# A query tile of sixteen heads, asked for once instead of once per head

## Chip, cores and metric

One core of a Trainium2 chip runs the kernel. The metric is the device time of one execution in microseconds (us), as the median of three runs. Lower is better.

## What is computed

The reference is a two-layer backbone over 1024 latent tokens (plus 256 context tokens) of width 1024. Layer 0 mixes neighbourhood attention with mLSTM heads. Layer 1, the last one, is a bidirectional gated linear recurrence (HGRN2) of 16 heads with key and value width 128. Cut to one direction of one head of layer 1, in chunks:

```
b = cumsum(lf)                       # lf = log(f), f the forget gate; k = 1 - f
o = (q * exp(b)) @ S                 # what the state carried into the chunk gives
a = einsum(q, exp(b_t - b_s) * k)    # pairs inside the chunk, s <= t
o = o + a @ v
S = exp(b_last) * S + (k * exp(b_last - b)).T @ v
```

The two directions are added, normalised per head, multiplied by a SiLU gate and projected back.

## The kernel before, in words

Everything is float32. A projection is split into a high and a low part and takes three TensorE matmuls per product (lines 131 to 133, in `dense`).

Layer 1 is a loop over 16 heads (lines 1443 to 1460). A head h consists of these pieces:

- `hg_intra` (from line 1027) makes, from the gates F and the query halves q, the tile K = 1 - F (line 1031), the two sums of keys (1036) and the **query tile Q** (1038). Q has 128 partitions and two rows of 1024 tokens, one for each direction. Four VectorE products fill it: for the token half `hf` = 1 (tokens 512 to 1023) and then `hf` = 0 (tokens 0 to 511), two directions each. Then come seven levels (`hg_level`): TensorE reads Q and keys in strips of 64 by 64 (line 1059), and VectorE multiplies parts of Q and K in place by the gate products (line 1106). The keys of a level are first copied by ScalarE into gksel (line 1089).
- `hg_vz` projects values and the gate z, `hg_close` transposes the keys, `hg_ctx` makes the states that the context leaves.
- `hg_scan` walks over eight chunks c of 128 tokens. For each chunk TensorE adds three matmuls into a PSUM tile "acc": line 1137 with the within-chunk matrix gA, lines 1138 and 1139 with the 128 columns of chunk c of the two rows of Q. VectorE then makes the next forward state (line 1144). After each group of four chunks, ScalarE squares the result (1153), VectorE multiplies it by z into the same columns of gA (1157), and GpSimd normalises (1158).
- `hg_proj` of the next head projects its gates and queries; `hg_out` transposes and stores the result. A few heads also do small sums on GpSimd (`wo_sums`, `y_diff`).

After the loop comes an output projection, whose weights arrive over SyncE's DMA queue.

Tiles come from pools with `self.t(pool, shape, dtype, tag, bufs)` (line 55). A request under a tag with one buffer gets the memory of the earlier tile of that tag only when every instruction that uses the earlier tile is through. Inside one tile the framework keeps account of which instructions read and write which part, and orders those that overlap.

The order of the instructions on each engine isn't written out by hand. The framework plans it while it builds the program, from a model of how long each instruction takes (`schedule_with_timeline_sim=True` in the launch): at each point an engine is given the ready instruction of the best priority. Priority follows the program's order, except that what stands under `urgent()` (the strips and the in-place products of the levels) goes ahead of everything. On the chip each engine then runs its list in that fixed order and waits where an operand isn't there.

Of the kernel before, what the change touches and what calls it, by code (L numbers as in the profile page):

```python
# [10 lines left out]
F32 = mybir.dt.float32  # L11
# [8 lines left out]
P = 128  # L20
D = 1024
KD = D // P
LAT = 1024
# [22 lines left out]
class Prog:  # L46
# [980 lines left out]
    def hg_intra(self, h, st, pool):  # L1027
        nc = self.nc
        F, q = st["F"], st["q"]
        K = self.t(pool, [P, 2, LAT], F32, "gK", 1)  # L1030
        nc.vector.tensor_scalar(out=K, in0=F, scalar1=-1.0, scalar2=1.0, op0=ALU.mult, op1=ALU.add)
        Q = self.t(pool, [P, 2, LAT], F32, "gQ", 1)
        ks = [self.t(pool, [P, 512], F32, "gkn", 4) for _ in range(2)]
        for hf in (1, 0):
            s = slice(hf * 512, (hf + 1) * 512)
            nc.vector.tensor_tensor(out=ks[hf], in0=K[:, 0, s], in1=K[:, 1, s], op=ALU.add)
            for d in range(2):
                nc.vector.tensor_tensor(out=Q[:, 1 - d, s], in0=q[hf], in1=F[:, d, s], op=ALU.mult)
        hv = dict(Q=Q, K=K, T=F, D=self.t(pool, [P, 8, 64], F32, "gD", 1))
        hv["A"] = self.t(pool, [P, 8, P], F32, "gA", 1)  # L1040
        if h == 0:
            self.t(pool, [P, 16], F32, "pad", 1)
        pa = self.ps("s", [P, 8, 64])
        with self.urgent():
            for c in range(8):
                for b in range(2):
                    o = c % 4 * P + b * 64
                    self.strip(pa[:, c, :], b, ks[c // 4][:, o : o + 64], q[c // 4][:, o : o + 64])
        nc.vector.tensor_tensor(
            out=hv["D"], in0=pa, in1=self.lmask[:, 0, :].unsqueeze(1).to_broadcast([P, 8, 64]), op=ALU.mult  # L1050
        )
        for lev in range(7):
            self.hg_level(hv, lev, pool)
        return hv
# [23 lines left out]
    def hg_level(self, H, lev, pool):  # L1078
        nc = self.nc
        n, h = LAT, 1 << lev  # L1080
        nb = n // (2 * h)
        K, Q, A, D, Tt = H["K"], H["Q"], H["A"], H["D"], H["T"]

        pick = lambda t: _skew(t[:, 0, :].rearrange("p (b s i) -> p b s i", s=2, i=h), 2, n)
        out = self.ps("s", [P, 8, 64])
        with self.urgent():
# [5 lines left out]
            for c in range(8):  # L1092
                for b in range(2):
                    o = c * P + b * 64
                    r = out[:, c, :]
                    if lev < 6:
                        r = r.rearrange("p (b s i) -> p b s i", s=2, i=h)
                        lhsT, rhs = ksel[:, o : o + 64], pick(Q)[:, o // (2 * h) : (o + 64) // (2 * h)]
                    else:
                        lhsT = K[:, b, o : o + 64]  # L1100
                        rhs = Q[:, 1 - b, c * P + (1 - b) * 64 : c * P + (2 - b) * 64]
                    self.strip(r, b, lhsT, rhs)
            for t, o, step in ((Q, n + 1, -n - 1), (K, 1, n - 1)):
                v = bass.AP(t.tensor, t.offset, [list(t.ap[0]), [n + h, 2], [2 * h, nb], [1, h]])
# [673 lines left out]
```

## Time and profile before

| | us |
|---|---|
| median of 3 runs | 3375.06 (3374.84 to 3375.25) |
| the profiled execution | 3376.8 |
| its span, first to last instruction | 3375.0 |
| TensorE (PE) busy | 3321.0 |
| VectorE (DVE) busy | 2022.1 |
| ScalarE (ACT) busy | 1402.1 |
| GpSimd (POOL) busy | 661.2 |

The profile is of one execution. PEld is the loading of weights into TensorE, which runs beside the matmuls. A row of a timeline gives the start and the length in us, the engine, the line of the kernel, the operation, what it writes and reads, how many instructions are merged into the row, and in brackets how long the engine was idle before and what it had waited for. Matmuls are pipelined: a row that says 0.28 us may be followed by the next start after 0.11 us. Layer 1's heads run from about 1839 to 3260 us.

### The profile page before, as it was taken

How to read it: one execution, taken by the hardware profiler on the slowest of the kernel's cores; microseconds unless marked ns; L12 is line 12 of the kernel's file. 1: busy time of each engine (PE TensorE's matmuls, PEld its weight loads, DVE VectorE, ACT ScalarE, POOL GpSimd, SP SyncE). 2: the span in 40 equal slices, each digit the busy share in tenths (PEclk: the TensorE clock that was granted, in tenths of full speed). 3: DMA queues.
4: the chain of work that ended last, by engine and by line, in shares of the span. 5: the costliest groups of instructions: out<-in, count | busy, mean ns of one | idle time of the engine just before them, and what ended most of it. 6: DMA issues, size and time to landing. Idle time of an engine off the chain costs nothing. (4 is left out here: it accounts for less than half of the span.)

```text
span 3375.0 us, 64228 instructions
## 1 busy us (share of the span) xinstructions
PE 3321.0 (98%) x24982; PEld 2940.1 (87%) x24982; DVE 2022.1 (60%) x4791; ACT 1402.1 (42%) x3310; POOL 661.2 (20%) x1059
## 2 busy tenths in 40 slices
PE   6999999999999999999999999999999999999999
PEld 5689999888989888898888999988899999989877
DVE  4437666666655566787656555555555555555557
ACT  5335544555544444454454333333333333333343
POOL 2222222222211112221100111122112222321110
PEclk8999999999999999999999999999999999999999
DMA  6622222232233434444652122122122322222366
GB/s 217 234 85 75 80 77 76 76 91 84 71 90 102 147 119 127 131 137 139 215 170 89 45 70 67 60 65 66 62 66 67 79 60 60 76 73 64 79 178 184
DMA packets 315696, 342.02 MB, mean 101 GB/s; under 512 B 32168, under 2 KB 257128, under 8 KB 313344
## 3 DMA queue, kind: packets, MB, share of 16 engines
q1 hardware_dynamic: 269520, 217.85, 21.9%
q0 software_dynamic: 45872, 120.07, 11.6%
q8 instruction: 197, 3.23, 0.4%
q14 instruction: 107, 0.88, 0.1%
HBM read 253.43 MB, written 84.21 MB: 100 GB/s over the span
## 5 line engine op out<-in xcount | busy, mean ns | idle before, releaser
L131 PE MATMUL mm<-hh,wh 128*128 128x512 f32 (+1 forms) x1600 | 583.2, 365 | 0.7 <-ACT gF L958 0.7
L132 PE MATMUL mm<-hl,wh 128*128 128x512 f32 (+1 forms) x1600 | 582.2, 364 | 0.0
L133 PE MATMUL mm<-hh,wl 128*128 128x512 f32 (+1 forms) x1600 | 581.5, 364 | 0.0
L131 PE MATMUL mm<-wh,hh 128*128 128x256 f32 (+1 forms) x1440 | 445.7, 310 | 2.5 <-DVE graw L300 1.4
L132 PE MATMUL mm<-wl,hh 128*128 128x256 f32 (+1 forms) x1440 | 444.7, 309 | 0.0
L133 PE MATMUL mm<-wh,hl 128*128 128x256 f32 (+1 forms) x1440 | 441.9, 307 | 0.0
L131 PEld LDWEIGHTS mm<-hh,wh 128*128 128x128 f32 x1600 | 301.6, 189 | 48.7 <-issue 2.5
L133 PEld LDWEIGHTS mm<-hh,wl 128*128 128x128 f32 x1600 | 301.4, 188 | 44.6 <-issue 0.2
L132 PEld LDWEIGHTS mm<-hl,wh 128*128 128x128 f32 x1600 | 301.7, 189 | 42.1 <-issue 0.2
L131 PE MATMUL mm<-wzh,hh 128*128 128x256 f32 x1024 | 294.5, 288 | 0.0
L133 PE MATMUL mm<-wzh,hl 128*128 128x256 f32 x1024 | 292.0, 285 | 0.0
L132 PE MATMUL mm<-wzl,hh 128*128 128x256 f32 x1024 | 290.2, 283 | 0.0
L131 PEld LDWEIGHTS mm<-wh,hh 128*128 128x128 f32 x1440 | 271.3, 188 | 21.1 <-ACT ev L322 3.4
L132 PEld LDWEIGHTS mm<-wl,hh 128*128 128x128 f32 x1440 | 271.3, 188 | 12.4 <-issue 0.7
L133 PEld LDWEIGHTS mm<-wh,hl 128*128 128x128 f32 x1440 | 271.2, 188 | 12.0 <-issue 0.5
L74 DVE TENSOR_TENSOR wl<-wraw,wh 128x512 fp32r<-128x512 f32 x240 | 167.7, 703 | 159.1 <-ACT wh L73 157.6
L73 ACT CAST wh<-wraw 128x512 fp32r<-128x512 f32 x240 | 147.2, 618 | 226.6 <-PE mm L132 167.2
L131 PEld LDWEIGHTS mm<-wzh,hh 128*128 128x128 f32 x1024 | 193.4, 189 | 2.5
L132 PEld LDWEIGHTS mm<-wzl,hh 128*128 128x128 f32 x1024 | 193.4, 189 | 1.6
L133 PEld LDWEIGHTS mm<-wzh,hl 128*128 128x128 f32 x1024 | 192.9, 188 | 1.2
L1089 ACT COPY gksel<-gK 128x1024 f32<-128x1024 f32 x96 | 110.8, 1154 | 163.9 <-PE s L1059 118.6
L1106 DVE TENSOR_TENSOR gQ<-gQ,gF 128x1024 f32<-128x1024 f32 x112 | 139.9, 1249 | 45.8 <-PE s L1059 44.8
(467 smaller groups left out, 7411.8 us busy)
## 6 DMA issues: line engine op xcount, KB each, us to landing
wraw<-in_wab_dram SPq DMA_DIRECT2D x108, 256.0 KB
wraw<-in_wc_dram SPq DMA_DIRECT2D x96, 256.0 KB
wraw<-yd SPq DMA_DIRECT2D x92, 256.0 KB
wraw<-in_wc_dram SPq DMA_DIRECT2D x128, 128.0 KB
md<-ev POOLq DMA_DIRECT2D x60, 256.0 KB, 2.7
mloz<-md SPq DMA_DIRECT2D x40, 256.0 KB
s<-gyt POOLq DMA_DIRECT2D x36, 256.0 KB, 4.3
adar<-in_wada_dram SPq DMA_DIRECT2D x8, 1024.0 KB
```

The costliest lines, as they stand in the source:

```text
L73: m = nc.scalar.copy(hi, x)
L74: nc.vector.tensor_tensor(out=lo, in0=x, in1=hi.bitcast(F32), op=ALU.subtract)
L131: mm(ps, lhsT=lh(k), rhs=rh(k), start=(start and k == 0), stop=False)
L132: mm(ps, lhsT=lh(k), rhs=rl(k), start=False, stop=False)
L133: m = mm(ps, lhsT=ll(k), rhs=rh(k), start=False, stop=(stop and k == nk - 1))
L1089: m = nc.scalar.copy(ksel.rearrange("p (b s i) -> p b s i", s=2, i=h), pick(K))
L1106: nc.vector.tensor_tensor(out=v, in0=v, in1=tot, op=ALU.mult)
```

## The change

Head 0 asks for the tile under the tag gQ and keeps it in `self.Q`; the other 15 heads use the same tile instead of asking for a new one. No instruction is added or taken away, and the memory is the same one buffer. What differs is on what the first writes of a head depend: not on the end of every use of the tile before, but on the earlier uses of the part that they write.

```diff
         nc.vector.tensor_scalar(out=K, in0=F, scalar1=-1.0, scalar2=1.0, op0=ALU.mult, op1=ALU.add)
-        Q = self.t(pool, [P, 2, LAT], F32, "gQ", 1)
+        if h == 0:
+            self.Q = self.t(pool, [P, 2, LAT], F32, "gQ", 1)
+        Q = self.Q
         ks = [self.t(pool, [P, 512], F32, "gkn", 4) for _ in range(2)]
         for hf in (1, 0):
             s = slice(hf * 512, (hf + 1) * 512)
             nc.vector.tensor_tensor(out=ks[hf], in0=K[:, 0, s], in1=K[:, 1, s], op=ALU.add)
             for d in range(2):
                 nc.vector.tensor_tensor(out=Q[:, 1 - d, s], in0=q[hf], in1=F[:, d, s], op=ALU.mult)
```

## The prediction

> **What bounds the kernel now.** I read the page first: the span and the busy times.
>
> ```profile
> span 3375.0 us, 64228 instructions
> PE 3321.0 (98%) x24982; PEld 2940.1 (87%) x24982; DVE 2022.1 (60%) x4791; ACT 1402.1 (42%) x3310; POOL 661.2 (20%) x1059
> ```
>
> TensorE (PE) is busy 3321.0 of 3375.0 us, so its idle time is 54 us in all. The change neither adds nor removes a matmul. What it can win is therefore at most the part of this idle time that the query tile causes. The table by stretches, for two of the sixteen heads and for one stretch of the last stage, says how much is left inside a head.
>
> ```profile
> 2278.06:2365.84 87.78, 87.15 (x781) 79.30 (x780) 49.98 (x82) 29.25 (x61) 18.23 (x27) 1.00 0.22 70
> 2365.84:2453.63 87.79, 87.17 (x781) 79.32 (x780) 50.08 (x81) 29.48 (x61) 18.32 (x27) 1.00 0.21 66
> ...
> 3280.00:3300.00 20.00, 16.27 (x59) 12.49 (x58) 9.12 (x15) 7.38 (x13) 1.17 (x2) 0.83 1.05 308
> ```
>
> The columns are the stretch, its length, the busy time of PE, PEld, DVE, ACT and POOL, then the clock granted to PE. A head takes 87.8 us, with PE idle for 87.79 - 87.17 = 0.62 us and the clock full. VectorE (DVE) is busy 50 us of it and has 37.7 us to spare. The list of waits, for PE from 1830 us to the end (the heads and the last stage), names what PE waited for:
>
> ```profile
> PE s L1059 <- DVE gQ L1038: 7.2, 12, 0.7
> PE c L131 <- ACT yh L73: 3.7, 1, 3.7
> PE mm L893 <- ACT yh L73: 1.5, 1, 1.5
> PE mm L131 <- ACT gF L958: 0.7, 1, 0.7
> PE c L131 <- DVE gA L1157: 0.6, 1, 0.6
> ```
>
> The first row is the query tile: 12 times, 7.2 us in total, the strips of level 0 waited for the four products that fill Q (line 1038). That is 0.6 us each, the same 0.62 us as in the table. The other rows have nothing to do with the tile. So 7.2 us, or 0.21% of the time, is the stall that this edit addresses. What those products themselves wait for is shown by the answer for the tile gQ:
>
> ```profile
> L1038 DVE TENSOR_TENSOR gQ<-gq,gF x64: 679/685/695, 1839.2 to 3170.8; 128x512 f32<-128x512 f32 x64
> its engine sat idle before it (us, times) until:
>   PE acc L1139: 38.9, 15
> ```
>
> There are 64 products, 4 for each head. In all 15 heads but the first, DVE sat idle (38.9 us in total, 2.6 us each) until line 1139 of the head before had been computed, that is until the scan had read Q for its last chunk.
>
> **The change part by part.** One boundary between heads, in DVE's timeline:
>
> ```profile
> 2368.40 0.35 DVE L1144 SCALAR_TENSOR_TENSOR gS<-gS,gT,s 128x128 f32<-128x128 f32 x1 [1.25 <-PE acc L1139]
> 2369.77 0.35 DVE L1144 SCALAR_TENSOR_TENSOR gS<-gS,gT,s 128x128 f32<-128x128 f32 x1 [1.02 <-PE acc L1139]
> 2371.76 0.69 DVE L1157 TENSOR_TENSOR gA<-acc,gz 128x512 f32<-128x512 f32 x1 [1.65 <-ACT gjk L1153]
> 2373.60 0.69 DVE L1049 TENSOR_TENSOR gD<-s,glm 128x512 f32<-128x512 f32 x1 [1.14 <-PE s L1059]
> 2374.46 0.35 DVE L1144 SCALAR_TENSOR_TENSOR gS<-gS,gT,s 128x128 f32<-128x128 f32 x1 [0.16 <-PE acc L1139]
> 2375.13 0.35 DVE L1144 SCALAR_TENSOR_TENSOR gS<-gS,gT,s 128x128 f32<-128x128 f32 x1 [0.32 <-PE acc L1139]
> 2378.06 2.50 DVE L1038 TENSOR_TENSOR gQ<-gq,gF 128x512 f32<-128x512 f32 x4 [2.58 <-PE acc L1139]
> ```
>
> and in PE's:
>
> ```profile
> 2369.34 0.39 PE L1139 MATMUL acc<-gS,gQ 128*128 128x128 f32 x2
> ...
> 2377.19 0.39 PE L1137 MATMUL acc<-gv,gA 128*128 128x128 f32 x2
> 2377.41 0.39 PE L1138 MATMUL acc<-gS,gQ 128*128 128x128 f32 x2
> 2377.63 0.39 PE L1139 MATMUL acc<-gS,gQ 128*128 128x128 f32 x2
> 2377.78 0.37 PE L131 MATMUL mm<-wzh,hh 128*128 128x256 f32 x1
> ...
> 2379.80 0.28 PE L133 MATMUL mm<-wzh,hl 128*128 128x256 f32 x1
> 2380.70 1.55 PE L1059 MATMUL s<-gQ,gksel 128*64 128x64 f32 x32 [0.62 <-DVE gQ L1038]
> ```
>
> The line 1139 at 2369.34 belongs to chunk 3, that at 2377.63 to chunk 7. Between lie 8.3 us in which columns 0 to 511 of Q are already read for the last time, but the products for them stand behind the last one all the same.
>
> *Is a part of a tile really freed alone?* The trace says so for gA, which is asked for once in each head. Line 1157 writes its first four chunks at 2371.76, while line 1137 still reads its last one at 2377.19: they overlap in nothing, and neither waits for the other. So I take it that with Q kept, the two products of tokens 0 to 511 need only chunk 3, and the two of tokens 512 to 1023 need chunk 7 as now.
>
> *What moves.* Per head, two of four DVE products. DVE's idle stretches before 2378.06 are 1.65, 1.14 and 2.58 us; the four products take 2.50 us, so two take about 1.25. They fit. Nothing else moves by the edit alone: no DMA is issued, no tile of another tag changes its place, and head 0 is as before. The strips of level 0 can then be planned some 1.2 us earlier, and the projection matmuls that stood before them come after them. For PE this is an exchange without price.
>
> *What is gained.* The gap of 0.62 us is an error of the plan: it put about 2.0 us of matmuls (2378.06 to 2379.80, plus 0.28) between the last read of Q and the strips, and the chain on the chip took 2.64 (2378.06 to 2380.70: products 2.50, handing over 0.14). With two products left behind chunk 7, the chain is about 1.25 + 0.14 = 1.39 us. If the plan covers the same share of it as now, 2.02 / 2.64 = 0.77, it puts 1.06 us of matmuls there and a wait of 0.33 us is left. The gain is 0.62 - 0.33 = 0.29 us, times 12 heads = **3.5 us**. The bounds: if the plan's error sits in handing over and not in the products, the wait stays as it is and nothing is won; if the error vanishes with the queue, all 7.2 us go. I take the middle value, since it is scaled from the row of the same operations, and keep both ends. What is late next inside a head is nothing that the waits show: beyond the 0.62 us PE has no idle time there.
>
> *What hides the moved products.* They stand in DVE's queue in the scan. Behind them wait line 1144 (the state, for which line 1139 of the next chunk on PE waits) and line 1157. They cost nothing as long as DVE is idle there anyway, as the rows in brackets show. If one starts just ahead of a 1144, it delays it by up to 0.6 us, and both by 1.25. PE then has the value projection's matmuls to run, unless its fixed order has the scan next.
>
> A row speaks of another price: GpSimd and DVE side by side.
>
> ```profile
> 2381.61 1.04 POOL L1158 TENSOR_TENSOR gA<-gA,gss 128x512 f32<-128x512 f32 x1
> ```
>
> ```profile
> 2382.29 1.45 DVE L1106 TENSOR_TENSOR gQ<-gQ,gF 128x1024 f32<-128x1024 f32 x1 [0.47 <-PE s L1059]
> ...
> 2388.66 1.21 DVE L1106 TENSOR_TENSOR gQ<-gQ,gF 128x1024 f32<-128x1024 f32 x1
> ```
>
> The same product takes 1.45 us where it begins under a GpSimd operation and 1.21 elsewhere. The products that move into the scan can meet the first half's 1158 in the same way. At 0.24 us each, that is at most 0.5 us a head, off PE's path as long as the scan has slack. The Trainium skill, "SBUF — State Buffer", section "Who interferes with whom", has a rule for this: a DVE instruction with two SBUF inputs contends with a GpSimd instruction that reads SBUF, and one of them fully blocks. By it the DVE product could lose the whole rest of the GpSimd operation; the trace shows a loss, but a smaller one than the 0.36 us of overlap that is left at 2382.29.
>
> **The sum.** The profiled execution took 3376.8 us, of which 1.8 lie outside its span; it is 1.7 us above the median of the runs. I take the 3.5 us off the median: 3375.1 - 3.5 = **3371.6 us**.
>
> **The rivals.**
>
> *The wait halves (forecast, 0.40).* As worked out: 3368.5 to 3374.8, likeliest 3371.6.
>
> *The whole bubble goes (0.22).* The plan, with half of the products out of the way, lets PE go on without a gap. Then 7.2 us go: 3367.9, and a little less if the last stage happens to fall better, down to about 3362. For it: the gap is the same 0.6 us in head after head. Against it: nothing in the trace says that the plan errs less on a shorter chain. The Trainium skill, "Perfetto Trace Analysis", section "Identifying the Most-Contended Engine", takes such a gap, repeating on the engine that should be saturated, as a possible sign that there isn't room for the next tile to be allocated. By that rule the whole gap is the tile's and would vanish. The trace agrees in that the gap's products wait for the old tile's last use.
>
> *Nothing happens (0.15).* The order stays, or the wait of the strips hangs on the last product alone. 3375, give or take 1.
>
> *The moved products get in the scan's way (0.18; slower).* The place is DVE's queue between 2369 and 2378 us of this head, the price up to 2 products = 1.25 us a head. It decides from the point at which a product starts less than 0.6 us ahead of a line 1144 whose matmul is next in PE's order. The stretches before 2374.46 and 2375.13 are only 0.16 and 0.32 us long, which speaks for it; the 1.14 to 2.58 us of the others speak against. Fully paid in 15 heads it is 19 us, 3394; for half, 3384. To this case belongs that the plan, made anew, interleaves scan and projections worse.
>
> *The last stage falls differently (0.05).* PE waits 3.7 us once near 3289 (second row of the waits), and in the stretch around it the clock granted is 0.83. Another arrival of the last head can take this away or double it: 4 us either way, so 3368 to 3383 with the rest.
>
> **How the numbers follow.** About 0.2% (6.75 us) is what a measurement of this kernel can tell from no change. Faster by more means below 3368.3: most of the second rival and a little of the forecast, 0.25. Slower by more means above 3381.8: most of the fourth and a little of the last, 0.19. Within: 0.56. The likeliest case's own range is 3368.5 to 3374.8. The range for 8 in 10 reaches to the whole bubble below (3364) and to about half the price of the slower rival above (3384).
>
> **What would show it.** In the changed profile, two of line 1038's products should start right after chunk 3's line 1139, and two after chunk 7's; DVE's idle time before 1038 should fall below 38.9 us. The wait of line 1059 for 1038 should be some 3.5 us in total instead of 7.2, and a middle head last 87.5 us. If the wait is gone altogether, the second rival is right; if all four products still stand together, the third; if waits of PE on 1144 appear or a head takes over 88 us with no more idle time, the fourth. I am wrong from the ground up if heads change by more than 1 us without a change in these waits: then the planner's new order, and not the tile, makes the time.

## The result, and the profile after

The changed kernel takes 3369.36 us (median of 18 runs, 3366.92 to 3374.73), the kernel before 3376.86 us beside it (18 runs, 3374.11 to 3380.89). The ratio is 0.9979, with an interval of 0.9972 to 0.9986: some 7.1 us, or 0.21%, are gone. The forecast was 3371.6 us for a kernel at 3375.1, that is 3.5 us less; the range of 3364 to 3384 held the time. On the chip the whole bubble went, which the prediction had as its second rival at 0.22.

The lines of the changed kernel stand two higher from the products on (the products are line 1040 here, the strips 1061, the scan's matmuls 1139 to 1141, the state 1146). Its profiled execution took 3371.7 us. First its page, span and busy times:

```profile
span 3370.0 us, 64226 instructions
PE 3321.2 (99%) x24982; PEld 2942.5 (87%) x24982; DVE 2032.7 (60%) x4791; ACT 1400.2 (42%) x3310; POOL 660.7 (20%) x1059
```

TensorE does the same work in the same busy time (3321.2 against 3321.0), so what is gone was idle time. VectorE is busy 10.6 us more, with as many instructions as before; the last section tells why. PE's waits from 1830 us on, after:

```profile
PE c L131 <- ACT yh L73: 4.1, 1, 4.1
PE c L131 <- DVE gA L1159: 0.6, 1, 0.6
PE mm L131 <- ACT lasth L73: 0.5, 1, 0.5
PE tr L1073 <- DVE gK L1108: 0.3, 1, 0.3
```

The row with 7.2 us in 12 waits has no successor. No strip waits for the query tile any more. The table by stretches (before the first product of head 0, from there to the first product of head 15, and the rest) says where the span became shorter. Before:

```profile
0.00:1839.21 1839.21, 1803.96 (x12044) 1574.77 (x12045) 1129.73 (x3349) 875.99 (x2234) 365.57 (x640) 1.00 0.39 120
1839.21:3169.02 1329.81, 1322.64 (x11815) 1204.16 (x11814) 754.68 (x1221) 441.73 (x914) 270.11 (x389) 1.00 0.22 64
3169.02:3375.00 205.98, 194.40 (x1127) 161.15 (x1125) 137.72 (x223) 84.40 (x163) 25.56 (x31) 0.98 0.63 173
```

and after:

```profile
0.00:1841.34 1841.34, 1802.56 (x12045) 1574.13 (x12046) 1131.09 (x3349) 875.59 (x2234) 366.67 (x640) 0.99 0.39 120
1841.34:3161.23 1319.89, 1319.63 (x11770) 1201.71 (x11768) 765.39 (x1224) 439.56 (x912) 269.02 (x389) 1.00 0.23 65
3161.23:3370.00 208.77, 199.05 (x1172) 166.70 (x1170) 136.24 (x220) 85.02 (x165) 24.96 (x31) 0.98 0.63 171
```

In the heads PE was idle 1329.81 - 1322.64 = 7.17 us before and 1319.89 - 1319.63 = 0.26 us after. The stretch is 9.92 us shorter: 6.91 of idle time, and 3.01 us of work, 45 PE instructions that the new order runs behind it. The last stretch is 2.79 us longer for them. Both together: 7.13 us less. The first stretch, in which nothing was edited, came out 2.13 us longer in this execution. The last section shows as much between kernels whose TensorE order is the same, so it is taken for chance; it is why the two spans differ by 5.0 us only.

One boundary between heads, DVE's timeline after:

```profile
2364.36 0.35 DVE L1146 SCALAR_TENSOR_TENSOR gS<-gS,gT,s 128x128 f32<-128x128 f32 x1 [1.13 <-PE acc L1141]
2364.81 0.69 DVE L1040 TENSOR_TENSOR gQ<-gq,gF 128x512 f32<-128x512 f32 x1
2365.85 0.35 DVE L1146 SCALAR_TENSOR_TENSOR gS<-gS,gT,s 128x128 f32<-128x128 f32 x1 [0.35 <-PE acc L1141]
2366.11 0.69 DVE L1040 TENSOR_TENSOR gQ<-gq,gF 128x512 f32<-128x512 f32 x1
...
2373.95 1.29 DVE L1040 TENSOR_TENSOR gQ<-gq,gF 128x512 f32<-128x512 f32 x2 [2.30 <-PE acc L1140]
```

Two products now stand in the scan, one ahead of a state product (1146) and one behind it, and only two come after chunk 7. PE at the same place:

```profile
2373.75 0.39 PE L1141 MATMUL acc<-gS,gQ 128*128 128x128 f32 x2
2373.90 0.36 PE L133 MATMUL mm<-wzh,hl 128*128 128x256 f32 x1
...
2377.02 1.58 PE L1061 MATMUL s<-gQ,gksel 128*64 128x64 f32 x32
```

Between chunk 7 and the strips stand 25 matmuls of the value projection, from 2373.90 to 2377.02, so 3.1 us; before, there were 18 in 2.3 us (2377.78 to 2380.08, of which 2.02 lie beside the products), and a gap. The last product ends at 2373.95 + 1.29 = 2375.24. The strips have no wait in brackets, and 1.6 us of slack beyond the hand-over of 0.14. So two things changed at once: the **chain** behind chunk 7 became shorter (two products instead of four), and the **cover** beside it became longer (25 matmuls instead of 18). Which of them took the bubble away is what the experiments had to tell.

### The profile page after: what moved, and what is told of

Read it like the earlier page. It is cut to its first block, busy times and chain, and to the rows that moved or that the text cites. A ratio compares the mean times of both kernels' runs of the same rounds, so it can differ in the third digit from the quotient of the medians.

```text
span 3370.0 us, 64226 instructions
## 1 busy us (share of the span) xinstructions
PE 3321.2 (99%) x24982; PEld 2942.5 (87%) x24982; DVE 2032.7 (60%) x4791; ACT 1400.2 (42%) x3310; POOL 660.7 (20%) x1059
```

## The experiments

Each kernel's ratio is to the kernel before on the same chip, over 11 runs (where not said otherwise), with its interval. The expectations speak of two theories. **A**: a strip's wait is the chain of products that it needs, less the work that the plan has beside it, and the early start of two products brings the chain below that cover. **B**, the prediction's own step: the plan covers a fixed share (0.77) of whatever chain there is. Where an expectation names a further theory (C, D, E), it says what that is. Lines move by a few in each kernel; the products are always the row `gQ<-gq,gF`.

### late: the kept tile, with the early products held back

```diff
             for d in range(2):
-                nc.vector.tensor_tensor(out=Q[:, 1 - d, s], in0=q[hf], in1=F[:, d, s], op=ALU.mult)
+                m = nc.vector.tensor_tensor(out=Q[:, 1 - d, s], in0=q[hf], in1=F[:, d, s], op=ALU.mult)
+                if hf:
+                    last = m
+                else:
+                    self.behind(m, last)
```

`behind` orders an instruction after another one on the same engine. The products of tokens 0 to 511 are put behind the product that fills row 0 of tokens 512 to 1023 (`d` = 1); the other late product stays free.

> The tile is kept, but its two products of tokens 0 to 511 are queued behind the first product of tokens 512 to 1023, so none starts before the last chunk of the scan. Theory A (the wait is the chain of products behind the last chunk minus the matmuls that the plan has ready to put beside it): the chain is again four products, 2.6 us, and from the fifth boundary on only 18 or 19 matmuls, 2.1 to 2.2 us, stand beside it, so PE waits some 0.5 us at 11 boundaries and the time is that of the kernel before, 0.999 to 1.001 of it. Theory C (keeping the tile is itself what helps, by a new plan): 0.998, as in the changed kernel.

Measured: 3369.79 us, 0.9983 (0.9975 to 0.9992). The bubble stayed away, against A as it was worked out. DVE in a middle head of this kernel:

```profile
2552.50 2.50 DVE L1040 TENSOR_TENSOR gQ<-gq,gF 128x512 f32<-128x512 f32 x4 [2.37 <-PE acc L1144]
```

and PE:

```profile
2554.78 1.54 PE L1065 MATMUL s<-gQ,gksel 128*64 128x64 f32 x32
```

All four products are late again, as intended. But the strips start at 2554.78, while the four end only at 2555.00. The edit had changed something else too: one late product now comes last, and only the second half of the strips needs it. In the program the wait is split: the first eight strips wait for three products, the next eight for the fourth. The kernel before has one wait, on all four, for all sixteen strips. The changed kernel has the split wait too: its plan puts row 1 of tokens 512 to 1023 last. The **order** of the products is thus a second possible cause, which neither theory had. `late` therefore doesn't speak for B either, and its result is what theory C gave; `strict` below decides on C.

### early1: one early product instead of two

```diff
-                nc.vector.tensor_tensor(out=Q[:, 1 - d, s], in0=q[hf], in1=F[:, d, s], op=ALU.mult)
+                m = nc.vector.tensor_tensor(out=Q[:, 1 - d, s], in0=q[hf], in1=F[:, d, s], op=ALU.mult)
+                if hf:
+                    last = m
+                elif d == 1:
+                    self.behind(m, last)
```

> As the changed kernel, but only one product may start early; three stand behind the last chunk. Theory A: the chain is 1.9 + 0.14 = 2.0 us, beside it stand 30 matmuls, 3.5 us, so no wait is left and the whole gain is there: 0.998 of the kernel before. Theory B (the prediction's: a fixed share, 0.23, of whatever chain is left is waited for): 0.47 us at 12 boundaries remain, 5.6 us, so the gain is only 1.6 us: 0.9995.

Measured: 3368.04 us, 0.9976 (0.9967 to 0.9985), and no wait of a strip. DVE and PE at a boundary:

```profile
2368.67 1.89 DVE L1040 TENSOR_TENSOR gQ<-gq,gF 128x512 f32<-128x512 f32 x3 [2.40 <-PE acc L1144]
```

```profile
2372.20 1.55 PE L1065 MATMUL s<-gQ,gksel 128*64 128x64 f32 x32
```

The products take 1.89 us, with the hand-over 2.03. By B, 0.23 of it would stay as a wait, 0.47 us a head. There is none: the products end at 2370.56, the strips come 1.6 us later, behind 30 matmuls. B falls with this run. Between early1 and the change (0.9979) no difference can be told.

### dup2: the kept tile, late products done twice

```diff
             for d in range(2):
-                nc.vector.tensor_tensor(out=Q[:, 1 - d, s], in0=q[hf], in1=F[:, d, s], op=ALU.mult)
+                for _ in range(2 if hf else 1):
+                    nc.vector.tensor_tensor(out=Q[:, 1 - d, s], in0=q[hf], in1=F[:, d, s], op=ALU.mult)
```

The second product of a pair writes the same numbers again. The chain behind chunk 7 has four products, as before the change, but the early two stay early.

> As the changed kernel with two products early, but the two late products are each done twice (the same numbers written again), so four stand behind the last chunk. Theory A: chain and matmuls as in the kernel before, 2.6 against some 2.2 us from the fifth boundary on, so PE waits about 0.5 us at 11 boundaries: 0.999 to 1.001. If the early start itself were what helps (theory C), the gain stays: 0.998. Theory B gives 1.000 as well.

Measured: 3368.89 us, 0.9978 (0.9969 to 0.9987), without a wait of the strips. Behind chunk 7 the row is again 2.50 us long. As in `late`, the last of the four is needed by the second half of the strips alone, and the wait is split. A as it was worked out (0.999 to 1.001) missed here too, for the same reason as in `late`. The run told nothing that `late` hadn't: with the order free, four products behind chunk 7 do no harm.

### strict: the kept tile, with all four products in the old order

```diff
+        last = None
...
-                nc.vector.tensor_tensor(out=Q[:, 1 - d, s], in0=q[hf], in1=F[:, d, s], op=ALU.mult)
+                m = nc.vector.tensor_tensor(out=Q[:, 1 - d, s], in0=q[hf], in1=F[:, d, s], op=ALU.mult)
+                if last:
+                    self.behind(m, last)
+                last = m
```

> The tile is kept, but the four products are chained on VectorE in the order that they have in the kernel before, tokens 512 to 1023 first, so that all four run behind the last chunk and the two that the first strips of level 0 read come last. The order of the instructions on TensorE comes out the same as in the kernel before. Theory A (the strips wait for the last of the products that they read, less the matmuls that the plan has ready beside it): 12 waits of 0.6 us as before, 1.000. Theory C (keeping the tile is what helps): 0.998.

Measured: 3376.3 us, 0.9998 (0.9989 to 1.0007). PE's waits in the heads:

```profile
PE s L1065 <- DVE gQ L1041: 7.2, 12, 0.7
```

The 7.2 us are back in 12 waits, to the tenth. Keeping the tile does nothing by itself. What it does is to let products move, and this run takes the moving away. It is the control that `late` should have been.

### swap: a tile per head, tokens 0 to 511 first

```diff
+        for hf in (0, 1):
+            s = slice(hf * 512, (hf + 1) * 512)
             for d in range(2):
                 nc.vector.tensor_tensor(out=Q[:, 1 - d, s], in0=q[hf], in1=F[:, d, s], op=ALU.mult)
```

> The query tile is asked for once per head as in the kernel before; only the order of its four products is turned, tokens 0 to 511 first. TensorE's order of instructions is that of the kernel before. The strips of level 0 go through tokens 0 to 511 first. Theory A: their first half needs two products, 1.29 + 0.14 = 1.43 us behind the last chunk, against 2.0 us of matmuls beside it, and the second half needs four, 2.64, against 2.0 and the 0.7 us of the strips' first half: no wait is left, all 7.2 us are won, 0.998. Theory D (the wait hangs on the whole tile, or on the number of products behind the last chunk): 12 waits of 0.6 us, 1.000.

Measured: 3376.45 us, 0.9999 (0.999 to 1.0008), and the same wait:

```profile
PE s L1061 <- DVE gQ L1040: 7.2, 12, 0.7
```

The expectation was that strips of the first tokens could go ahead of the late half. They couldn't: in the program all sixteen strips of level 0 have one wait, on the product that comes last, which here writes row 0 of tokens 512 to 1023. Which products the first strips are made to wait for can be seen only by comparing this order with the next one.

### order: a tile per head, the products in the new order alone

```diff
-            for d in range(2):
-                nc.vector.tensor_tensor(out=Q[:, 1 - d, s], in0=q[hf], in1=F[:, d, s], op=ALU.mult)
+        last = None
+        for hf, d in ((1, 1), (0, 0), (0, 1), (1, 0)):
+            s = slice(hf * 512, (hf + 1) * 512)
+            m = nc.vector.tensor_tensor(out=Q[:, 1 - d, s], in0=q[hf], in1=F[:, d, s], op=ALU.mult)
+            if last:
+                self.behind(m, last)
+            last = m
```

> The query tile is asked for once per head as in the kernel before, and all four products stand behind the last chunk; only their order is changed: row 0 of tokens 512 to 1023 first, then the two of tokens 0 to 511, row 1 of tokens 512 to 1023 last. In the program the first half of the strips then waits for the first three products and the second half for the fourth, where the kernel before waits for all four ahead of the first strip. Theory A: three products take 1.89 + 0.14 = 2.03 us against 2.0 to 2.1 us of the 18 or 19 matmuls beside them, so at most 0.1 us is waited for, and the fourth runs beside the first strips: some 7 us are won without a kept tile, 0.998. Theory C (the kept tile, or the early start that it allows, is needed): 1.000.

Measured: 3372.18 us, 0.9988 (0.9979 to 0.9997). No strip waits, although all four products stand behind chunk 7 and no tile is kept. PE has another wait in its place:

```profile
PE mm L131 <- DVE gz L994: 1.5, 7, 0.2
```

That is the value projection behind the strips: its next group of matmuls needs a PSUM buffer that the product of line 994 frees, and this stands behind the four products in DVE's queue. About 4 us of the 7 are won by the order alone (1 to 7 by the interval). The strips of tokens 0 to 511 don't read row 0 of tokens 512 to 1023, and yet they wait for it in `swap` and don't wait for row 1 of these tokens here; why the framework counts so wasn't looked into.

### earlyd: the kept tile, two products early, the late ones in the old order

```diff
-            for d in range(2):
-                nc.vector.tensor_tensor(out=Q[:, 1 - d, s], in0=q[hf], in1=F[:, d, s], op=ALU.mult)
+        last = None
+        for hf, d in ((0, 0), (0, 1), (1, 0), (1, 1)):
+            s = slice(hf * 512, (hf + 1) * 512)
+            m = nc.vector.tensor_tensor(out=Q[:, 1 - d, s], in0=q[hf], in1=F[:, d, s], op=ALU.mult)
+            if last:
+                self.behind(m, last)
+            last = m
```

Here the strips have the single wait of the kernel before, so that only the early start is left.

> The tile is kept and the two products of tokens 0 to 511 start early, but the two late ones are put into the order that they have in the kernel before, so that the first strips need both of them. Theory A: the chain behind the last chunk is 1.29 + 0.14 = 1.43 us, beside it stand 18 to 32 matmuls, at least 2.0 us: no wait is left, 0.998. If the split of the strips' wait were what helps in the changed kernel, and not the early start, the 0.6 us at some 10 boundaries would stay: 1.000.

Measured: 3368.85 us, 0.9978 (0.9969 to 0.9987), with no wait of a strip. DVE at a boundary:

```profile
2369.80 1.28 DVE L1042 TENSOR_TENSOR gQ<-gq,gF 128x512 f32<-128x512 f32 x2
...
2377.89 1.29 DVE L1042 TENSOR_TENSOR gQ<-gq,gF 128x512 f32<-128x512 f32 x2 [2.59 <-PE acc L1146]
```

and PE:

```profile
2377.61 0.37 PE L133 MATMUL mm<-wzh,hl 128*128 128x256 f32 x1
...
2379.95 1.55 PE L1066 MATMUL s<-gQ,gksel 128*64 128x64 f32 x32
```

This is the cleanest boundary of all. The cover is nearly that of before: 19 matmuls in 2.34 us, where there were 18 in 2.30; from the first late product on, 2379.95 - 2377.89 = 2.06 us, where there were 2.02. The chain has gone from 2.64 to 1.29 + 0.14 = 1.43 us. The wait is gone. It is so at ten boundaries, with 18 or 19 matmuls each; at the first five this plan has 32. So the early start alone is enough for the whole gain, and it needs no longer cover.

The four runs that separate the two causes, as ratios to the kernel before:

| | late products in the old order | in the new order |
|---|---|---|
| all four behind chunk 7 | strict 0.9998 | late 0.9983, order 0.9988 (no kept tile) |
| two of them early | earlyd 0.9978 | the change 0.9979 |

Either cause takes the strips' wait away, and both together do no more than the early start alone. By their intervals, `order`, `late` and `earlyd` can't be told from each other; what separates them is the wait on line 994 in `order`.

### bdup: a tile per head, the products of tokens 0 to 511 done twice

```diff
             for d in range(2):
-                nc.vector.tensor_tensor(out=Q[:, 1 - d, s], in0=q[hf], in1=F[:, d, s], op=ALU.mult)
+                for _ in range(1 if hf else 2):
+                    nc.vector.tensor_tensor(out=Q[:, 1 - d, s], in0=q[hf], in1=F[:, d, s], op=ALU.mult)
```

The opposite of the change: the chain has six products instead of four.

> The kernel before, with the two products of tokens 0 to 511 done twice (the same numbers written again), so six products, about 3.7 + 0.14 = 3.85 us, stand behind the last chunk. TensorE's order has 61, 61, 21, 11, 29, 11, 35, 11, 22, 12, 21, 12, 12, 22, 22 matmuls between the last chunk and the strips at the 15 boundaries, at 0.112 us each. Theory A: the waits of the strips for the products add up to 23 us in place of 7.2, the time grows by 16 us, 1.005. Theory E (such a wait is only moved from one place to another, since TensorE makes up for it later): no change beyond 0.1%.

Measured: 3421.75 us (4 runs), 1.013 (1.0114 to 1.0145), so 45 us more, nearly three times what A gave (16 us). The waits:

```profile
PE tr L1197 <- POOL gA L1159: 29.5, 10, 4.0
PE s L1060 <- DVE gQ L1039: 10.0, 3, 3.3
```

The strips' own wait grew only to 10.0 us, in three places. At ten others the plan has put the transposes of the output (line 1197) ahead of the strips, and PE waits there instead. The product by z isn't held up at these ten: it starts 2.73 us behind the start of chunk 7's last matmul, as at most boundaries of the kernel before. What A had wrong is the chain. DVE at a boundary with the longest of these waits:

```profile
2751.92 2.50 DVE L1039 TENSOR_TENSOR gQ<-gq,gF 128x512 f32<-128x512 f32 x4 [2.61 <-PE acc L1140]
2754.34 0.68 DVE L1158 TENSOR_TENSOR gA<-acc,gz 128x512 f32<-128x512 f32 x1
2754.94 0.42 DVE L1008 TENSOR_SCALAR gq<-gFc 128x512 f32<-128x512 f32 x1
2755.27 2.13 DVE L1039 TENSOR_TENSOR gQ<-gq,gF 128x512 f32<-128x512 f32 x2
```

The six products end at 2757.40, 5.48 us after the start of the first and not 3.7. The plan has two other instructions between them, and the last product took 1.53 us beside GpSimd's line 1159 (2755.47 to 2756.85). The chain is 4.64 or 5.48 us at every boundary, and the two rows of waits add up to 39.5 us, where A had 23. The rest of the loss isn't waiting. The heads' stretch, and then a wait and the stretch behind it:

```profile
1839.13:3211.47 1372.34, 1335.52 (x11809) 1213.53 (x11808) 775.81 (x1250) 438.31 (x913) 272.75 (x388) 0.99 0.22 62
```

```profile
2389.02:2392.36 3.34, 0.01 (x1) 0.04 (x1) 3.34 (x7) 0.75 (x5) 2.85 (x4) 1.00 0.21 79
2392.60:2396.00 3.40, 3.40 (x40) 3.28 (x36) 2.15 (x3) 1.54 (x2) 0.51 (x1) 0.50 0.00 0
```

PE is busy 12.9 us longer in the heads than before (1335.52 against 1322.64) with as many instructions, and behind the wait its granted clock is half. So waits make 32.3 us of the loss (39.5 against 7.2), and the 12.9 us go with the lower clock. The sign of A was right and E is out; A's size was wrong, because it took the chain for the products alone and counted no time beyond the waits.

### keepz: the gate tile kept instead of the query tile

```diff
-        z = self.t(pool, [P, NT - 2, P], F32, "gz", 1)
+        if h == 0:
+            self.z = self.t(pool, [P, NT - 2, P], F32, "gz", 1)
+        z = self.z
```

This asks what held the cover at 18 matmuls before. The z product (994) of the next head needs the old gate tile, which is free only after the last product by z of the scan (1157), behind the four products. If that is the limit, keeping gz lets PE run on.

> The kernel before, with the query tile asked for once per head as there; instead the gate tile z is kept for all heads, so that its products need not wait for the last read of the old z, which stands behind the four query products, and the PSUM buffers of the value projection come free earlier. Theory A: the plan no longer runs out of matmuls and puts 42 to 45 of them, about 5 us, beside the chain of 2.6 us; the waits of the strips for the query products vanish, the gain is some 7 us without a change of Q, 0.998, and a little less if the fewer changes between kinds of matmuls count. Theory B: the chain of products is as long as before, so the 7.2 us of waits stay: 1.000.

Measured: 3379.94 us, 1.0012 (1.0003 to 1.0021): slightly slower. The cover did grow, to 44 or 45 matmuls at every boundary, and the strips of level 0 no longer wait for their products. The cap is thus confirmed. The heads' stretch of the profile is 5.75 us shorter than before (1324.06 against 1329.81), but the stretch behind it is 6.4 us longer (212.39 against 205.98):

```profile
PE s L1061 <- ACT gksel L1091: 6.1, 2, 3.4
PE acc L1139 <- DVE gA L1159: 2.6, 3, 0.9
PE s L1061 <- DVE gQ L1108: 1.9, 1, 1.9
```

The first and the last row, 8.0 us, fall into the last head. The likely reason, not tested, is that the value projection that was run early is missing there: nothing is left to run beside the levels. Behind the first of these waits (3.36 us) the granted clock is 0.50 for 13.6 us. Two kept tiles in one kernel, and a second buffer for the query tile, weren't tried; for the second buffer (8 KB in each partition) there is no room.

## Why the prediction was right, and where it failed

**What bounds the kernel: right.** PE's idle time inside the heads was the stall of 7.17 us, and nothing else inside them was to be won.

**A part of a tile is freed alone: right.** The row of DVE at 2364.81 is the first product of a new head, written while the scan still reads later tokens. DVE's idle time before the products, after the change:

```profile
L1040 DVE TENSOR_TENSOR gQ<-gq,gF x64: 682/686/1530, 1841.3 to 3161.8; 128x512 f32<-128x512 f32 x64
...
  PE acc L1140: 34.2, 15
```

It fell from 38.9 to 34.2 us, as was asked for, but by little: the wait for chunk 7 remains before the late pair.

**What moves: right in part.** Two products move into the scan. They did not start together right behind chunk 3, but one at a time around a state product (1146), and neither delays it: DVE is idle for 0.35 us ahead of the one at 2365.85. "The strips of level 0 can then be planned some 1.2 us earlier" was wrong: they come 3.1 us behind chunk 7, later after it than before (2.9 us, from 2377.78 to 2380.70), and more of the projection runs ahead of them. For PE this is the same: it has work all the time.

**What is gained: this step failed.** "If the plan covers the same share of it as now, 2.02 / 2.64 = 0.77" is the sentence. The cover was never a share of the chain, nor the gap an error of the plan. The cover was 17 to 19 matmuls at the 12 boundaries with a wait because there the value projection ran out of PSUM buffers, for a reason that keepz shows: the z product behind the four products. (At the first three boundaries the kernel before has 44, 44 and 38 matmuls with the same chain, and no strip waits; why the plan had more there wasn't tried.) That length need not shrink when the chain becomes shorter. With the cover of 2.02 us left as it was and the chain at 1.43 us, the wait would have come out at nothing; earlyd, with a cover of 2.34, shows just this. In the change the cover even grew. So all 7.2 us go and not 3.5. The numbers for that sum were in the prediction; scaling the cover with the chain was the error. That 3369.36 us lies within the forecast's own 3368.5 to 3374.8 is luck: the kernel before came out at 3376.86 beside it and not at 3375.06. The difference, 7.1 us by the ratio, is twice the forecast's 3.5.

The second rival had the right size, 3367.9 of 3375.1, against the 7.1 us measured. The Trainium skill, "Perfetto Trace Analysis", section "Optimization Strategy" (the prediction named the section ahead of it), had stood beside it: a gap that repeats on the engine that should be saturated can mean that there isn't room for the next tile. The runs agree in part: with one tile in the same memory, the gap goes once two products needn't wait for the old tile's last use (`earlyd`). But `order` closes it too, with a tile per head, by the order of the products alone.

**The slower rival: didn't happen.** The scan's PE waits on line 1146 appear nowhere. The heads in the middle take 87.33 us, below the 87.5 of the forecast:

```profile
2373.95:2461.29 87.34, 87.34 (x781) 79.55 (x779) 50.52 (x82) 29.20 (x61) 18.06 (x28) 1.00 0.21 67
```

PE is busy in all 87.34 us. Before it was 87.17 busy and 0.62 idle, so 0.17 us of the 0.62 came back as busy time. The new order changes between kinds of matmuls twice more often in a head (58 times against 56), which may be it; this wasn't tried.

**The last stage: the rival didn't happen.** The stage took 2.79 us more, but with 45 more PE instructions from the heads, and its one long wait was neither taken away nor doubled: 4.1 us instead of 3.7.

**GpSimd beside DVE: too small.** The prediction put it at 0.24 us for a product, off PE's path. Off the path it is; the size is in the last section.

## What to carry to other kernels

Here a wait of the bounding engine was the chain that its next instruction needed, less the work that stood ready beside it. Find what ends that work (here another tile's release, stuck in the same queue) and take it as a length, not as a share of the chain. The length belongs to one plan: another edit can make it longer (25 matmuls in the change, 18 before). Keeping a tile instead of asking again changes nothing by itself; it pays where a part of the tile is read for the last time well before the whole, and its writers then really start earlier. Before an experiment on order is read, look at the order that the program got and at which products each reader is made to wait for: an edit that holds something back can change that too, as `late` did.

## What the runs showed of the hardware

VectorE is busy 10.6 us more with the same instructions. The row of one line explains nearly all of it. Line 1008 before:

```profile
L1008 DVE TENSOR_SCALAR gq<-gFc x16: 411/417/427, 1845.2 to 3172.0; 128x512 f32<-128x512 f32 x16
```

and after:

```profile
L1008 DVE TENSOR_SCALAR gq<-gFc x16: 427/1125/1130, 1847.2 to 3156.5; 128x512 f32<-128x512 f32 x16
```

The median is 1.125 us instead of 0.417. Fourteen of the 16 take 0.95 to 1.13 us, together 9.3 us more than before; at one further boundary a product of the query tile takes 1.53 instead of 0.69. In the new order these 15 instructions meet a GpSimd instruction. At one boundary, GpSimd and then DVE of the changed kernel:

```profile
2369.03 1.04 POOL L1160 TENSOR_TENSOR gA<-gA,gss 128x512 f32<-128x512 f32 x1
```

```profile
2369.22 1.12 DVE L1008 TENSOR_SCALAR gq<-gFc 128x512 f32<-128x512 f32 x1 [0.88 <-PE s L1061]
```

GpSimd ends at 2370.07, DVE at 2370.34, 0.27 us later, of the 0.42 that it needs alone. An early product in dup2 does the same beside another GpSimd instruction:

```profile
2538.20 1.27 POOL L1189 TENSOR_TENSOR gknc<-gEc,gknc 128x512 f32<-128x512 f32 x1 [2.75 <-DMA gEc<-yd]
```

```profile
2538.63 1.40 DVE L1041 TENSOR_TENSOR gQ<-gq,gF 128x512 f32<-128x512 f32 x1
```

It ends at 2540.03, 0.56 us behind GpSimd's end at 2539.47, of the 0.69 that it needs alone. In both the instruction is held until GpSimd's ends, but for some 0.14 us that it has behind it by then; it is 0.14 in all 15 cases of the changed kernel. The row of the prediction fits the same account: GpSimd ended at 2382.65, the product at 2383.74, 1.09 us later of 1.21. The prediction read this row as a partial loss, since only 0.36 us of overlap were left there. The Trainium skill, "SBUF — State Buffer", section "Who interferes with whom", has such an instruction fully blocked if it has two SBUF inputs, as a product has, or runs in a mode with two ports, which a tensor_scalar can enter; which mode line 1008 ran in isn't shown. The runs agree but for that first tenth of a microsecond. A moved product can thus cost up to 0.84 us (1530 ns in the row of the tile against 686), not 0.24. Here DVE has the time to spare.

A long wait of PE cost more than its length. At the boundaries of `bdup`, PE has eleven waits of 2.79 to 3.99 us, and behind nine of them the granted clock is half for 3.4 to 6.8 us. Behind the two waits of 1.26 and 1.97 us it stays full, as it does behind the 0.4 to 0.7 us in the kernel before. Why two of the eleven go without isn't known. So the bubble that the change removes was worth its own length, while the waits of `bdup` cost a third as much again (12.9 us beside 39.5).

The time of a whole execution lies up to 2.8 us below and up to 5.4 us above its median (both kernels of the result, 18 runs each), against 7.1 us that the change is worth. Much of it arises ahead of the heads. The kernel before, `strict` and `swap` have the same order on TensorE and differ there: the first product of head 0 starts at 1839.2 us in the first, and in the others at

```profile
L1041 DVE TENSOR_TENSOR gQ<-gq,gF x64: 680/686/695, 1841.1 to 3171.6; 128x512 f32<-128x512 f32 x64
```

```profile
L1040 DVE TENSOR_TENSOR gQ<-gq,gF x64: 680/686/695, 1838.7 to 3169.9; 128x512 f32<-128x512 f32 x64
```

That is a difference of 2.4 us. From there to the end, the three take 1535.8, 1534.6 and 1535.3 us, which differ by 1.2, and the changed kernel takes 1528.7. For a change inside the heads, this part of one profile says more than its span.
